# Attention's reload in eight buffers, and branch B's product begun with three tiles in places of their own

## The chip, the cores and the metric

The kernel runs on one core of one Trainium2 chip. The metric is the device time of one execution in microseconds, as the median of repeated runs. Beside it stands one profiled execution, from which every row below is taken. The engines are TensorE (PE, with its weight loads as PEld), VectorE (DVE), ScalarE (ACT), GpSimd (POOL) and SyncE (SP), which issues most of the transfers.

## The reference

One step of a one-layer streaming encoder with 1024 features: 528 prompt tokens (16 of them learned) and 64 sample tokens, so T = 592 columns. A normalised input goes through one wide projection, then through two branches side by side, a gated merge and an MLP. The lines that matter:

```python
h = _rmsnorm(x, p["norm1"])
proj = h @ p["w_in"]          # q, k, v of attention | DeltaNet q, k, v | z | beta, decay | gates A, B
o_a = attend(qa, ka, va, lam) # differential attention, two softmax maps per head
o_a = (_rmsnorm(o_a, p["sub_norm"]) * (1.0 - lam_init)).reshape(bsz, t, A_V_WIDTH)
...
o_b, s_new = _gated_delta(qb, kb, vb, g, beta, ssm0.astype(f32))
z = jax.nn.silu(z_b.astype(f32)).reshape(bsz, t, B_HEADS, B_HEAD_DIM)
o_b = (_rmsnorm(o_b, p["gdn_norm"]) * z).reshape(bsz, t, B_WIDTH).astype(x.dtype)
y_a = o_a @ p["w_br_a"]
y_b = o_b @ p["w_br_b"]
mix = jax.nn.sigmoid(gate_a + p["b_gate"][0]) * y_a + jax.nn.sigmoid(gate_b + p["b_gate"][1]) * y_b
x = x + mix @ p["w_out"]
h2 = _rmsnorm(x, p["norm2"])
x = x + jnp.square(jax.nn.relu(h2 @ p["w_up"])) @ p["w_down"]
```

## The kernel before

**Layout and arithmetic.** Activations lie with features on the partitions: eight tiles (KC = 8, index kc) of 128 features by TQ = 576 columns. Every product is made in three terms: a weight and an activation are each split into a rounded high part and a remainder (`split`, L275: ScalarE casts the high part, VectorE subtracts for the low part), and high x high, high x low and low x high are accumulated. A product task of 256 output features (`feat`, L470) has four parts, two halves of the features by two halves of 288 columns. A part is 8 x 3 = 24 matmuls into one bank; PG = 3 banks of the tag `pg` are used in turn. After a part its `evac` reads the bank, and the bank is free for the next part but two.

**Order.** The instructions of each engine's queue are written in the order in which a planner emits them (`manual_schedule`). The planner `Pace` (L53) keeps an estimated time per engine. `stream` (L300) walks through the list of tasks and yields after every 8 matmuls; `drive` (L449) lets it take one such step, then lets each side chain (a generator) take a step if the planner holds its inputs for ready. A task starts only when its `need` holds. Stores are put off until the planner holds their source for ready, and all transfers of the stages below, except the tiles of x, go through SyncE's queue in order.

**The stages that the change touches.** The last tasks that read the normalised input `hh`, `hl` are the gate tasks `g00` to `g03` (`gate_tasks`, L1175): each part ends in a tanh on ScalarE (`gt`), stored to `th_d`. Attention's chains run beside them. `load_ob` (L1430) loads DeltaNet's output from `ob_d` into eight tiles `ma` as soon as DeltaNet is through, then waits for the mark "hidden" and splits all eight into the place of `hh` and `hl`, which nobody reads any more, and sets "ob". The task `g03` is given `last=("hidden", "ob")`: after its last product it sets "hidden" and holds until "ob" is set, and only then emits its outstanding tanh.

Then come four tasks `bb0` to `bb3` (`br_b_tasks`, L1445; product of DeltaNet's output with `w_br_b`, tile `pg_bb`). Their `evac` loads a gate tile `thb`, multiplies on VectorE and stores to `mb_d`. HELD = 3: `bb0` to `bb2` need "ob"; `bb3` needs "merge", which is set when all of attention's chains are through and its memory has been given back. Attention's finished heads lie in `oa_d` by then. `load_oa` (L1489) loads them again, tile after tile through SyncE, into a tag `oa` with two buffers, and splits each into `oh` and `ol`; then "oa" is set. Four tasks `ba0` to `ba3` (`br_a_tasks`, L1465, tile `pg_ba`) need "oa". Their `evac` loads `tha` and `mbr` (branch B's result) and adds, and splits the sum into `mxh`, `mxl`. The tag `gth` has three buffers for `gt`, `thb`, `tha` and `mbr` together.

`residual` (L1497) runs from the end of `bb3` on: for each of five tiles of x it issues a load through GpSimd into a tag `xt` with one buffer, waits for the planner's landing time and 4000 ns more, turns it on TensorE in two groups (`pxr`) and copies to `x1`. When `ba3` and `residual` are through, the task `o0` (tile `pg_o`, the product with `w_out`) may start.

## Time and profile before

| | us |
|---|---|
| median of 3 runs | 1315.92 (1314.86 to 1316.42) |
| the profiled execution | 1314.69 |
| its span, first to last instruction | 1312.9 |
| TensorE busy | 1277.6 (97%) |
| VectorE busy | 863.8 (66%) |
| ScalarE busy | 603.7 (46%) |
| GpSimd busy | 110.1 (8%) |
| mean granted clock of TensorE | 0.994 |

The profiled execution's own time is 1.79 us above its span. "Busy" of TensorE counts a matmul from its start to its modelled end, so two that overlap in the pipeline are counted once. A granted clock of 1.00 is 2.4 GHz, of 0.50 it is 1.2 GHz. A wait is put down to the releaser that came last. Nearly all instructions pass through one helper, so all have the line L165; they are told apart by their tiles.

### The profile page before, as it was taken

Reading aid. Unit: us, or ns where it says so; the run is one execution under the profiler, and the core shown is the slowest. Engines: PE = TensorE matmul, PEld = TensorE weight load, DVE = VectorE, ACT = ScalarE, POOL = GpSimd, SP = SyncE. Lnnn points to the kernel's source line nnn. Section 1 sums busy time; section 2 is a strip of 40 time slices with the busy share of each in tenths; the row PEclk is TensorE's granted clock in tenths of the full one; section 3 lists DMA queues with packets and bytes.
Section 4 is the critical chain, followed back from the end, with each engine's and each line's share of the span. In section 5 each row is a group of like instructions: output and inputs, shape, how many; then the busy total and the mean of one; then the engine's idle time right before and its main releaser. Section 6 shows DMA issues by size and latency. Waiting matters only on the chain.

```text
span 1312.9 us, 25759 instructions
## 1 busy us (share of the span) xinstructions
PE 1277.6 (97%) x10177; PEld 1236.2 (94%) x10177; DVE 863.8 (66%) x1887; ACT 603.7 (46%) x1421; POOL 110.1 (8%) x207
## 2 busy tenths in 40 slices
PE   7999999999999999999998997999999999999998
PEld 5989899999999999998887997999999999999998
DVE  5766899434477624557777864445678678678687
ACT  5565554333643343237676652233453453453442
POOL 3111423200021000000000001200000000000000
PEclk9999999999999999999999998999999999999999
DMA  6324144532654422676444435632232323323322
GB/s 164 96 68 154 56 132 127 157 94 64 204 171 131 140 85 68 186 218 206 143 149 149 157 122 203 213 107 82 68 94 90 105 64 97 113 60 99 100 77 77
DMA packets 167934, 160.48 MB, mean 122 GB/s; under 512 B 24587, under 2 KB 148765, under 8 KB 167814
## 3 DMA queue, kind: packets, MB, share of 16 engines
q1 hardware_dynamic: 165702, 153.04, 38.3%
q0 software_dynamic: 2112, 5.80, 1.5%
q8 instruction: 80, 1.31, 0.4%
q14 instruction: 40, 0.33, 0.1%
HBM read 123.94 MB, written 37.81 MB: 123 GB/s over the span
## 4 chain that ended last, share of the span: by engine, by line
PE 85%; DVE 6%; ACT 4%; DMA 3%; issue 1%; SPq 0%; POOL 0%; DVEq 0%; ACTq 0%; POOLq 0%
PE pg_u L165 16%; PE pg_a L165 11%; PE pg_d L165 9%; PE pg_g L165 7%; PE pg_ba L165 4%; PE pg_z L165 4%; PE pg_o L165 4%; PE pd_dn L165 4%; PE pa_dn L165 4%; PE pc_dn L165 4%; PE pg_bb L165 3%; PE ppo L165 2%; PE pb_dn L165 2%; ACT djk L165 2%; PE po L165 1%
## 5 line engine op out<-in xcount | busy, mean ns | idle before, releaser
L165 PE MATMUL pg_u<-h2h,wh_u 128*128 128x288 f32 x512 | 151.4, 296 | 0.0
L165 PE MATMUL pg_u<-h2h,wl_u 128*128 128x288 f32 x512 | 151.3, 296 | 0.0
L165 PE MATMUL pg_u<-h2l,wh_u 128*128 128x288 f32 x512 | 151.3, 296 | 0.0
L165 PE MATMUL pg_a<-wh_a,hh 128*128 128x256 f32 (+1 forms) x480 | 136.3, 284 | 0.1
L165 PE MATMUL pg_a<-wh_a,hl 128*128 128x256 f32 (+1 forms) x480 | 135.8, 283 | 0.0
L165 PE MATMUL pg_a<-wl_a,hh 128*128 128x256 f32 (+1 forms) x480 | 135.5, 282 | 0.0
L165 PE MATMUL pg_d<-hl,wh_d 128*128 128x336 f32 (+1 forms) x384 | 115.5, 301 | 0.3 <-DVE hl L165 0.3
L165 PE MATMUL pg_d<-hh,wh_d 128*128 128x336 f32 (+1 forms) x384 | 115.6, 301 | 0.0
L165 PE MATMUL pg_d<-hh,wl_d 128*128 128x336 f32 (+1 forms) x384 | 115.4, 301 | 0.0
L165 PEld LDWEIGHTS pg_u<-h2h,wh_u 128*128 128x128 f32 x512 | 96.1, 188 | 0.1
L165 PEld LDWEIGHTS pg_u<-h2l,wh_u 128*128 128x128 f32 x512 | 96.1, 188 | 0.0
L165 PEld LDWEIGHTS pg_u<-h2h,wl_u 128*128 128x128 f32 x512 | 96.1, 188 | 0.0
L165 PEld LDWEIGHTS pg_a<-wh_a,hh 128*128 128x128 f32 (+1 forms) x480 | 86.5, 180 | 0.8 <-ACT sq L165 0.3
L165 PEld LDWEIGHTS pg_a<-wh_a,hl 128*128 128x128 f32 (+1 forms) x480 | 86.6, 181 | 0.5 <-issue 0.3
L165 PEld LDWEIGHTS pg_a<-wl_a,hh 128*128 128x128 f32 (+1 forms) x480 | 86.5, 180 | 0.3 <-issue 0.2
L165 PE MATMUL pg_g<-hh,wl_g 128*128 128x288 f32 x256 | 77.1, 301 | 0.0
L165 PE MATMUL pg_g<-hh,wh_g 128*128 128x288 f32 x256 | 77.0, 301 | 0.0
L165 PE MATMUL pg_g<-hl,wh_g 128*128 128x288 f32 x256 | 76.8, 300 | 0.0
L165 PEld LDWEIGHTS pg_d<-hl,wh_d 128*128 128x128 f32 x384 | 72.4, 189 | 1.2 <-issue 0.6
L165 PEld LDWEIGHTS pg_d<-hh,wl_d 128*128 128x128 f32 x384 | 72.8, 189 | 0.7 <-issue 0.6
L165 PEld LDWEIGHTS pg_d<-hh,wh_d 128*128 128x128 f32 x384 | 72.5, 189 | 0.2
L165 ACT CAST wh_dn<-wr_dn 128x1024 fp32r<-128x1024 f32 x32 | 33.6, 1050 | 81.4 <-DVE wr_dn L165 41.2
(398 smaller groups left out, 3785.0 us busy)
## 6 DMA issues: line engine op xcount, KB each, us to landing
wr_u<-in_w_up_dram SPq DMA_DIRECT2D x32, 512.0 KB, 3.6
wr_dn<-in_w_down_dram SPq DMA_DIRECT2D x32, 512.0 KB, 3.7
wr_d<-in_w_in_dram SPq DMA_DIRECT2D x24, 512.0 KB, 5.6
wr_a<-in_w_in_dram SPq DMA_DIRECT2D x24, 512.0 KB, 3.9
wr_g<-in_w_in_dram SPq DMA_DIRECT2D x16, 512.0 KB, 4.7
at_d<-st SPq DMA_DIRECT2D x48, 128.0 KB, 2.4
th_d<-gt SPq DMA_DIRECT2D x16, 288.0 KB, 2.1
wr_z<-in_w_in_dram SPq DMA_DIRECT2D x8, 512.0 KB
```

Source lines behind the costliest of these rows:

```text
L165: r = f(*a, **kw)
```

## The change

Four things are changed.

- `load_oa`: the eight tiles `oa` have a buffer each, and all eight loads are issued at once through GpSimd's queue when the merge's memory is opened. The chain only splits, tile after tile.
- `load_ob` and `feat`: the first OWN = 3 tiles of DeltaNet's output are split into a new pool `own`, without waiting for "hidden"; only the other five wait for it. `bb0` is called with `lead=3`: it first emits the matmuls of these three tiles for three parts, in three banks, and then completes each part with the remaining five tiles.
- `feat`: an outstanding `evac` is emitted before a task sets its `last` mark and holds, not after. Only `g03` has such a mark among the tasks that use `feat`, so its last tanh stands ahead of the splits.
- `residual`: two buffers for the tiles of x, the next load is issued one tile ahead, and the first turning waits until the first two parts of `ba0` are evacuated.

```diff
--- before.py
+++ after.py
@@ -45,6 +45,7 @@
 SC = 3
 WT = 2
 HELD = 3
+OWN = 3
 MASKED = -32768.0
 
 THR = [0, 1, 2, 3, 4, 5, 6, 7, 8, 12, 16, 23, 32, 46, 64, 91]
@@ -467,18 +468,29 @@
                     c.ready, idle = r or pace.ready, 0
         pace.flush()
 
-    def feat(xh, xl, nm, evac, m=P, ms=(0, P), halves=QHALVES, after="start", last=None, turn=False):
+    def feat(xh, xl, nm, evac, m=P, ms=(0, P), halves=QHALVES, after="start", last=None, turn=False, lead=0):
 
         def body(w):
             parts, full = [(h, c) for h in range(len(ms)) for c in (halves[::-1] if turn and h else halves)], deque()
             if "start" not in done:
                 parts.sort(key=lambda x: x[1])
+
+            begun = {}
+            for h, (a, b) in parts[:PG if lead else 0]:
+                ps = begun[h, a] = pg.tile([P, 512], F32, name=f"pg_{nm}{h}{a}", tag="pg")
+                for kc in range(lead):
+                    for i, (ww, xx) in enumerate(((w[0], xh), (w[0], xl), (w[1], xh))):
+                        TE.matmul(ps[:m, :b - a], ww[:, kc, ms[h]:ms[h] + m], xx[kc][:, a:b], start=kc == i == 0, stop=False)
+                yield
             for h, (a, b) in parts:
                 while len(full) == PG:
                     yield False
-                ps = pg.tile([P, 512], F32, name=f"pg_{nm}{h}{a}", tag="pg")
-                n = 0
-                for kc in range(KC):
+                ps = begun.pop((h, a), None)
+                k0 = 0 if ps is None else lead
+                if not k0:
+                    ps = pg.tile([P, 512], F32, name=f"pg_{nm}{h}{a}", tag="pg")
+                n = 3 * k0
+                for kc in range(k0, KC):
                     for ww, xx in ((w[0], xh), (w[0], xl), (w[1], xh)):
                         xk = xx[kc] if isinstance(xx, list) else xx[:, kc]
                         TE.matmul(ps[:m, :b - a], ww[:, kc, ms[h]:ms[h] + m], xk[:, a:b], start=n == 0, stop=n == 3 * KC - 1)
@@ -486,12 +498,12 @@
                         if n % QUANTUM == 0 and n < 3 * KC:
                             yield
                 full.append((h, ps[:m, :b - a], a, b))
+                while full and after in done:
+                    evac(*full.popleft())
                 if last and h == len(ms) - 1 and b == TQ:
                     done.add(last[0])
                     while last[1] not in done:
                         yield False
-                while full and after in done:
-                    evac(*full.popleft())
                 yield
         return body
 
@@ -598,7 +610,7 @@
     hh = hp.tile([P, KC, T], F32R, name="hh")
     hl = hp.tile([P, KC, T], F32R, name="hl")
     hq, lq = (x[:, :, N0:T] for x in (hh, hl))
-    ob = [x[:, :, 0:TQ] for x in (hh, hl)]
+    ob = [[], []]
 
     def load_x(pl, t):
         xt = pl.tile([P, D], F32, name=f"x_s{t}", tag="xt")
@@ -1436,10 +1448,17 @@
             obs.append(ab_.tile([P, TQ], F32, name=f"ma{j}", tag="ob"))
             Q.dma_start(obs[j], ob_d[j][:, N0:T])
             yield
+        for j in range(OWN):
+            for o in ob:
+                o.append(late["own"].tile([P, TQ], F32R, name=f"own{j}{len(ob[0])}", tag=f"own{j}{len(o)}{o is ob[0]}"))
+            split(ob[0][j], ob[1][j], obs[j])
+            yield
         while "hidden" not in done:
             yield
-        for j in range(KC):
-            split(ob[0][:, j], ob[1][:, j], obs[j])
+        for j in range(OWN, KC):
+            for o, x in zip(ob, (hh, hl)):
+                o.append(x[:, j, 0:TQ])
+            split(ob[0][j], ob[1][j], obs[j])
         done.add("ob")
 
     def br_b_tasks():
@@ -1456,7 +1475,7 @@
                     store(mb_d[j], th)
 
             def body(w, c=c, evac=evac):
-                yield from feat(ob[0], ob[1], f"bb{c}", evac)(w)
+                yield from feat(ob[0], ob[1], f"bb{c}", evac, lead=OWN if c == 0 else 0)(w)
                 if c == 3:
                     done.add("br_b")
             out.append(Task(f"bb{c}", w_br_b[0], c * 256, body, has("ob") if c < HELD else has("merge")))
@@ -1476,6 +1495,7 @@
                 if b == TQ:
                     V.tensor_tensor(th, th, mb, ALU.add)
                     split(late["mxh"][j], late["mxl"][j], th)
+                    done.add(f"ba{j}")
 
             def body(w, c=c, evac=evac):
                 yield from feat(late["oh"], late["ol"], f"ba{c}", evac)(w)
@@ -1487,19 +1507,28 @@
     late = {}
 
     def load_oa():
-        for j in range(KC):
-            a = mg.tile([P, TQ], F32, name=f"oa{j}", tag="oa")
-            Q.dma_start(a, oa_d[j])
-            yield
+        for a in late["oa"]:
+            yield pace.free(a)
+            j = late["oa"].index(a)
             split(late["oh"][j], late["ol"][j], a)
         done.add("oa")
 
     def residual():
 
         x1 = late["x1"]
-        for t, (c0, n) in enumerate(QTILES):
-            xt = mg.tile([P, D], F32, name=f"x_r{t}", tag="xt")
-            G.dma_start(xt[:n], x_prompt[0, c0:c0 + n] if t < 4 else x_sample[0])
+        xts = deque()
+        for t in range(-1, NT):
+            if t < NT - 1:
+                c0, n = QTILES[t + 1]
+                xts.append(mg.tile([P, D], F32, name=f"x_r{t + 1}", tag="xt"))
+                G.dma_start(xts[-1][:n], x_prompt[0, c0:c0 + n] if t < 3 else x_sample[0])
+            if t < 0:
+
+                while "ba0" not in done:
+                    yield
+                continue
+            c0, n = QTILES[t]
+            xt = xts.popleft()
             yield pace.free(xt) + 4000
             for q in range(2):
                 pv = bank(f"pxr{t}{q}").rearrange("p (k c) -> p k c", k=4)
@@ -1686,6 +1715,8 @@
         chains += [Chain(delta(g)) for g in range(2)]
         chains.append(Chain(conv_out()))
         drive(lambda: not chains and has("delta0", "delta1")())
+    own_cm = pool("own")
+    late["own"] = own_cm.__enter__()
     with pool("attn", side="right") as at_:
         ab_ = Tags(pace, at_, qk=4, v=3, past=3, sc=SC, mx=6, wT=WT, ob=8, aoss=3, bias=2, osb=3,
                    aqT0=2, aqT1=2, akT0=2, akT1=2)
@@ -1697,12 +1728,16 @@
         for nm in ("mxh", "mxl"):
             late[nm] = [mp.tile([P, TQ], F32R, name=f"{nm}{j}", tag=f"{nm}{j}") for j in range(KC)]
         with pool("merge", side="right") as mg_:
-            mg = Tags(pace, mg_, oa=2, xt=1)
+            mg = Tags(pace, mg_, oa=8, xt=2)
+            late["oa"] = [mg.tile([P, TQ], F32, name=f"oa{j}", tag="oa") for j in range(KC)]
+            for j in range(KC):
+                G.dma_start(late["oa"][j], oa_d[j])
             for nm in ("oh", "ol"):
                 late[nm] = [mg.tile([P, TQ], F32R, name=f"{nm}{j}", tag=f"{nm}{j}") for j in range(KC)]
             done.add("merge")
             chains.append(Chain(load_oa()))
             drive(has("br_b"))
+            own_cm.__exit__(None, None, None)
             hp_cm.__exit__(None, None, None)
             xp = ctx.enter_context(pool("x1"))
             late["wx"] = Tags(pace, xp)
```

## Rows read from the trace of the kernel before

**Rows 1.** The page: the span; engines' busy time, share of it, instructions.

```profile
span 1312.9 us, 25759 instructions
...
PE 1277.6 (97%) x10177; PEld 1236.2 (94%) x10177; DVE 863.8 (66%) x1887; ACT 603.7 (46%) x1421; POOL 110.1 (8%) x207
```

**Rows 2.** Stretches, PE alone: from:to, length, busy (count), PEclk, DMA share, GB/s.

```profile
798.55:815.00 16.45, 8.80 (x36) 0.69 0.48 159
785.50:797.60 12.10, 12.10 (x93) 1.00 0.90 306
805.00:814.00 9.00, 5.36 (x16) 0.50 0.46 148
```

**Rows 3.** Timeline of SyncE (start, us, engine, line, what); the tile `oa`'s issues, ns min/median/max.

```profile
800.32 0.32 SPq L165 DMA_DIRECT2D mb_d<-thb  x1
800.74 7.53 SPq L165 DMA_DIRECT2D oa<-oa_d  x4
...
L165 SPq DMA_DIRECT2D oa<-oa_d x8: 319/410/1066, 784.1 to 807.9; - x8
```

**Rows 4.** Timeline of ScalarE and TensorE; in brackets the idle time before, and its releaser.

```profile
805.75 1.37 ACT L165 CAST oh<-oa 128x576 fp32r<-128x576 f32 x2 [5.70 <-DMA oa<-oa_d]
...
806.47 0.61 PE L165 MATMUL pg_ba<-oh,wh_ba 128*128 128x288 f32 x1 [4.92 <-ACT oh L165]
```

**Rows 5.** Stretches, PE alone, columns as in group 2.

```profile
705.95:721.10 15.15, 11.51 (x76) 0.89 0.42 130
592.00:705.90 113.90, 113.17 (x904) 1.00 0.51 162
709.00:712.00 3.00, 3.00 (x14) 0.50 0.01 2
```

**Rows 6.** Timeline of ScalarE, VectorE and TensorE, 704 to 720 us.

```profile
706.89 4.67 ACT L165 CAST hh<-ma 128x576 fp32r<-128x576 f32 x8
711.47 0.49 ACT L165 ACTIVATE gt<-pg_g,bgh 128x288 f32<-128x288 f32 x1
...
707.58 5.44 DVE L165 TENSOR_TENSOR hl<-ma,hh 128x576 fp32r<-128x576 f32 x8 [0.23 <-ACT hh L165]
...
707.60 0.40 PE L165 MATMUL pg_bb<-hh,wh_bb 128*128 128x288 f32 x1 [1.67 <-ACT hh L165]
719.31 0.33 PE L165 MATMUL ptk<-ident,k 128*128 128x128 f32 x1 [1.60 <-DVE mx L165]
```

**Rows 7.** Tile `x_r`: issues (ns min/median/max), landing; timeline of GpSimd at 786 us.

```profile
L165 POOL DMA_DIRECT2D x_r<-in_x_prompt_dram x4: 547/561/610, 788.5 to 835.2; - x4
...
DMA to landing us min/median/max: 3.9/4.7/4.8
...
786.21 2.40 POOL L165 TENSOR_TENSOR wl_ba<-wr_ba,wh_ba 128x1024 fp32r<-128x1024 f32 x1 [24.39 <-ACT wh_ba L165]
```

**Rows 8.** Chain of waits in order of time, 774 to 800 us: start, us, what.

```profile
782.20 0.64 PE pot L165 x5
782.84 8.76 PE pg_bb L165 x64
...
793.67 4.95 DMA thb<-th_d
```

**Rows 9.** Chain of waits, 818 to 866 us: turnings of x, the next product.

```profile
830.86 0.44 PE pxr L165 x4
...
844.53 0.44 PE pxr L165 x4
...
858.78 0.39 PE pxr L165 x4
...
865.76 0.27 PE pg_o L165 x2
```

**Rows 10.** Stretches, all engines: length, then PE, PEld, DVE, ACT, POOL busy (count), PEclk, DMA.

```profile
600.00:620.00 20.00, 19.84 (x160) 17.41 (x159) 15.26 (x52) 13.88 (x48) 0.61 (x4) 1.00 0.56 182
...
760.00:780.00 20.00, 19.87 (x157) 18.23 (x157) 14.12 (x56) 10.26 (x31) 0.15 (x1) 1.00 0.25 85
```

## Prediction

> **What bounds the kernel now.** I read the page first: TensorE is busy for 1277.6 of the 1312.9 us of the span [rows 1]. A part of this kernel is therefore worth what it takes away from TensorE's idle or slow time, and work of the other engines counts only where TensorE waits for it. Second, I looked with the view by stretches for places where TensorE's busy time or its granted clock falls below full. In the part that the diff touches there are two. From 798.55 to 815.00, where the product of branch A begins, there are 36 recorded matmuls in 16.45 us at a mean clock of 0.69, against 93 in 12.10 us just before [rows 2]. From 705.95 to 721.10, where the product of branch B begins, there are 76 matmuls in 15.15 us, against 904 in 113.90 us in the stretch before, with nearly the same mixture of a product and attention [rows 5]. Third, I read the timeline for what ended each wait.
>
> In the first place SyncE issues a store of `thb` at 800.32, and only behind it, at 800.74, the remaining reloads of the attention output; four issues take 7.53 us because each needs one of two buffers back from a split [rows 3]. ScalarE's split stands idle for 5.70 us until the transfer lands, and TensorE for 4.92 us until that split [rows 4]. The clock goes to 0.50 afterwards, which is the 1.2 GHz level, for about nine microseconds [rows 2]. In the second place ScalarE makes all eight splits in a row from 706.89 (4.67 us, 0.58 each) and VectorE their low parts from 707.58 (5.44 us, 0.68 each). TensorE has waited 1.67 us for the first, and the clock is 0.50 from 709 to 712. The last gate's tanh comes at 711.47, behind all of them. At 719.31 TensorE waits another 1.60 us for VectorE, which has not caught up [rows 5, 6].
>
> **The sum against the profiled execution.** It took 1314.69 us, which is the span of 1312.9 and 1.79 around it; it lies 1.23 us below the median of the runs shown, 1315.92. I take the gain from the profiled time and add these 1.23 us again.
>
> **Reload in eight buffers, issued by GpSimd.** A matmul of a clean stretch costs 12.10 / 93 = 0.130 us, so the 36 of the bad one should take 4.7 us, and 16.45 - 4.7 = 11.8 us are lost now [rows 2]. This includes the slow clock, which I therefore don't count again. The change removes the waiting for two buffers and takes eight issues out of SyncE's queue, where they stood behind the stores of branch B. It adds eight issues to GpSimd's queue at 0.56 us each, or 4.5 us; a load from that queue landed in 3.9 to 4.8 us [rows 7]. When do they start? At the earliest when the destination's memory is free; at the latest when attention's last output is stored. TensorE turns this last output until 782.8, and I allow 3.3 us for the copy and the store [rows 8]. From 786.1 the last of eight would be issued by 790.6 and landed by 795.4, and its two halves of the split (0.58 and 0.68) are done by 796.7. Branch A's product starts at 798.55 [rows 2]. So even the late case fits, with 1.9 us to spare, and the kc that needs the last split comes 21 matmuls (2.7 us) later. In the early case seven of eight land before attention ends. I take 11.5 us as the gain. The bounds are 12 and 6.5: the low one is a transfer of 4.95 us, as `thb` has now [rows 8], that would come back on the path.
>
> Queued behind the eight issues on GpSimd are one subtraction that makes low weights (`wl_ba`, 2.40 us at 786.21 [rows 7]) and the first load of x. SyncE's next load of weights waits for that subtraction, and a load of `thb` stands behind the load of weights. Up to 4.5 us of delay there is covered: the weights in question are those of the second of four steps, due 96 matmuls (12.5 us) after 798.55; a late `thb` holds a bank that is needed 24 matmuls (3.1 us) after 798.55. I cost it at nothing; uncovered it costs 4.5 - 3.1 = 1.4 us.
>
> A rule speaks against this part. The Trainium skill says (Trainium Kernel Development and Optimization, Key Constraints) that transfers issued from several engines share the same 16 DMA engines, and that issuing from another engine saves only the sequencer's issue time. By that rule the change of queue would win about 8 x 0.41 us of issuing [rows 3], so some 3.3 us in place of 11.5, and the time would be 1309.1. The trace agrees on the sharing (the share of 0.90 below) but not that the issue time is all: at 800.74 it is a store and a buffer that SyncE's queue waits for [rows 3].
>
> **Three tiles early, three banks, tanh first.** Counted with the 113.90 / 904 = 0.126 us per matmul of the mixed stretch, the 76 matmuls should take 9.6 us, so 15.15 - 9.6 = 5.5 us are lost [rows 5]: 1.67 of waiting for the first tile, about 2.2 of slow clock and small waits, 1.60 for VectorE. With three tiles split long before, 3 banks x 3 tiles x 3 matmuls = 27 matmuls (3.5 us) can run from 705.95. Meanwhile ScalarE ends its attention work at 706.9, makes the tanh (0.49) and five splits of 0.58: all high parts by 710.3. VectorE's five low parts end at about 711.4. TensorE reaches the fourth tile at about 709.5 and the last at 711.2; some 0.3 us of waiting stay. The third bank is freed by the tanh at about 707.4, and it is needed after 18 matmuls, at 708.3. So the first 3.9 us should go. The 1.60 us for VectorE need not: VectorE has 3 x 0.68 = 2.0 us less to do there, but TensorE arrives 3.9 us earlier, so this wait can also grow by 1.9 us. Gain between 5.5 + 0.5 (if attention is also served better) and 2.0; I take 3.5, nearer to the row with the remaining wait.
>
> The three splits go to the stretch in which DeltaNet's output is reloaded, near 600 to 620. There ScalarE is busy for 13.88 and VectorE for 15.26 of 20 us, with TensorE at 19.84 [rows 10]: 3 x 0.58 and 3 x 0.68 fit. I cost them at nothing; without that cover they cost 2 us. The matmuls stay the same in number, and moving tanh in `feat` changes no other task.
>
> **Residual after branch A's first step, two buffers.** Now a tile of x is turned every 13.7 us (830.86 to 844.53), and the last is turned at 858.78, 7 us before the next product starts at 865.76 [rows 9]. The change starts this later, after two parts of the first step (48 matmuls, 6.3 us), but loads a tile ahead. Only the transfer and the fixed delay in the order (4 us) are overlapped; I estimate a step of about 10 us, so 6.3 + 4 x 10 + 4 = 50 us, against 96 x 4 x 0.130 + 4 = 54 us for the product with its turning. It costs nothing then.
>
> The sum: 11.5 + 3.5 = 15.0 us. 1314.69 - 15.0 = 1299.7, and at the median of runs 1300.9.
>
> **Rivals.**
> - The start's gain is given back at the merge. Branch B's fourth step may not start before attention's chains are through. Now that is tight: attention's last turning ends at 782.84, and the fourth step, 96 x 0.130 = 12.5 us long and over by about 797.8, begins near 785.3, only 2.5 us later; 64 matmuls of branch B run without a break in between and behind [rows 8]. If attention goes at its own speed (VectorE is busy for 15.26 of 20 us near 600 [rows 10]), branch B's first three steps run out 3.5 us sooner and TensorE waits there instead. For it: 64 matmuls in a row show attention not ready, or through, for a long piece [rows 8]. Against it: VectorE has 2 us less to do. Time: 1304.4.
> - Transfers. From 785.5 to 797.6 the DMA engines are busy for 0.90 of the time [rows 2]. If the reloads don't start before attention's end, five of them (1.47 MB, 4.8 us at the 306 GB/s of that stretch) are added there, and `thb`, weights or `tha` come 5 us late on the path: 1305.9. Against it: from 760 to 780 the share is 0.25 [rows 10], and seven of eight outputs are stored by then. With the first rival together, 1309.4. The skill's rule above ends at the same place.
> - Slower: the residual becomes the bound. If a tile still takes 13.7 us, since what sets it may be the order and not the buffer, the last one is turned 6.3 + 4 x 13.7 + 4 = 65.1 us after the start, and the next product waits 11 us for it, with the slow clock behind that wait (nine microseconds at half speed cost 4.5). That takes away 15.6 us: 1316.5. With the 3.5 us of the first rival lost besides, it is slower: 1320. The residual decides from a step of 11 us per tile on.
> - The change doesn't do what it says: the early splits are placed late in the order, or the eight loads wait for memory on GpSimd until attention's last tiles are free. The second is the late case reckoned above and costs nothing. The first leaves the start as it is: 1304.4 again.
>
> **How the numbers follow.** Forecast, 1300.9 with 1297 to 1303 of its own: 0.58. Gain of the start lost in either way, 1304.4: 0.19. Transfers (with the page's rule, 1306 to 1309.5): 0.12. Residual as the bound: 0.11, half of it within the 0.2% (2.6 us, about what a measurement of this kernel can tell from no change) and half beyond. The range reaches from 1315.92 - 12 - 6 = 1297.9, taken down to 1297 because both losses are reckoned from recorded matmuls alone and a few records can be missing, to the joint case of 1309.5. Faster 0.89, same 0.05, slower 0.06.
>
> **What would show it.** Right: no row of `oa` in SyncE's queue; eight issues on GpSimd with all landings before branch B's last matmul; no wait of TensorE over 0.5 us at the first product of branch A; a granted clock of 1.00 in both places; 27 matmuls right behind the last gate, and the tanh ahead of five splits. Wrong: TensorE idle ahead of branch B's fourth step (the merge); a wait for `tha` or `thb`; the last turning of x just before `pg_o`; or a new wait near 600. If both places are clean and the time is still above 1305, the loss lies where I didn't look.

## The result, and the profile after

The changed kernel takes **1324.59 us** (median of 4 runs, 1321.59 to 1325.15) against 1315.80 of the kernel before beside it. The ratio is 1.0058, 95% interval 1.0036 to 1.0080: it is slower by 8.8 us, where 1300.9 was forecast. The profiled execution took 1321.59. The page of the changed kernel answers [rows 1]:

```profile
span 1319.8 us, 25749 instructions
...
PE 1282.1 (97%) x10177; PEld 1240.0 (94%) x10177; DVE 863.2 (65%) x1883; ACT 603.6 (46%) x1423; POOL 117.9 (9%) x217
```

The change touches only what lies between attention's first score matmul (`psc`) and the first matmul of `pg_o`. Three marks cut that into two stages: **stage A** from the first `psc` to the first `pg_ba` (gates, attention, branch B), **stage B** from there to the first `pg_o` (branch A). The view by stretches gives it for the kernel before, with the three stretches gates, branch B and branch A (columns: from:to, length, busy us and count of PE, PEld, DVE, ACT, POOL, then PEclk, DMA share, GB/s):

```profile
591.40:707.60 116.20, 113.81 (x912) 101.58 (x911) 88.03 (x327) 83.60 (x260) 5.16 (x36) 1.00 0.52 164
707.60:798.00 90.40, 88.16 (x673) 81.10 (x674) 63.94 (x213) 50.43 (x141) 4.89 (x16) 0.98 0.48 158
798.60:865.60 67.00, 59.35 (x419) 56.88 (x418) 29.23 (x41) 20.51 (x30) 13.70 (x8) 0.92 0.57 184
```

and for the changed kernel:

```profile
590.00:698.00 108.00, 105.36 (x838) 94.12 (x837) 78.35 (x275) 74.01 (x225) 4.25 (x30) 1.00 0.51 164
698.00:807.10 109.10, 100.12 (x748) 89.97 (x747) 75.15 (x263) 63.31 (x182) 12.94 (x31) 0.95 0.44 142
807.10:872.50 65.40, 58.68 (x426) 57.73 (x426) 27.84 (x40) 17.54 (x25) 15.21 (x9) 0.95 0.59 193
```

Stage A grew by 9.9 us (207.2 to 217.1), stage B fell by 1.6 only (67.0 to 65.4); what follows takes 447.3 us in both, and the first `psc` came 1.4 earlier (591.4, 590.0). 9.9 - 1.6 - 1.4 = 6.9 us, the difference of the two spans. The gates' stretch became 8.2 us shorter, but only since 74 recorded matmuls left it; 75 more stand in branch B's, which takes 18.1 us more (the line of before ends 0.6 us short of the first `pg_ba`). There TensorE is idle for 9.0 us (2.2 before), and its clock is 0.95 (0.98 before). Over all of stage A idle time grew by 7.0 us (4.6 to 11.6). The other 2.9 us are longer busy time of nearly as many recorded matmuls, at a lower mean clock.

**The start** is as forecast. TensorE's timeline at the end of the gates has no wait left; the tiles `own` follow attention's matmuls directly (before: 1.67 us [rows 6]):

```profile
696.52 0.61 PE L166 MATMUL ppo<-v,wT 128*128 128x128 f32 x4
697.06 1.00 PE L166 MATMUL psc<-akT,aqT 64*128 64x264 f32 x12
697.98 0.53 PE L166 MATMUL pg_bb<-own,wh_bb 128*128 128x288 f32 x2
```

**The merge's wait** is new. From 767 to 792 attention is alone on TensorE, since branch B's first three steps are used up and the fourth may not begin (`pwT` turns the softmax weights, `ppo` multiplies them by v, `pot` turns the finished output):

```profile
769.30 1.23 PE L166 MATMUL pwT<-ident,sc 128*128 128x128 f32 x5 [1.88 <-DVE sc L166]
...
778.35 1.01 PE L166 MATMUL pwT<-ident,sc 128*128 128x128 f32 x7 [0.95 <-DVE mx L166]
...
781.71 1.83 PE L166 MATMUL ppo<-v,wT 128*128 128x128 f32 x14 [1.46 <-ACT wT L166]
...
790.86 1.38 PE L166 MATMUL pot<-ident,osb 128*128 128x128 f32 x5 [2.54 <-DVE osb L166]
```

Where [rows 8] had 64 matmuls of branch B without a break, TensorE now waits for softmax steps one by one. The last turning (`pot`) ends at 792.2, before at 782.8.

**The reload** has moved its wait. GpSimd's timeline, then SyncE's, VectorE's and TensorE's, answer [rows 3, 4]:

```profile
787.47 2.12 POOL L166 DMA_DIRECT2D oa<-oa_d  x4 [9.99 <-PE ppo L166]
795.43 0.54 POOL L166 DMA_DIRECT2D oa<-oa_d  x1 [5.84 <-DMA oa_d<-oaT]
800.05 0.54 POOL L166 DMA_DIRECT2D oa<-oa_d  x1 [4.08 <-DMA thb<-th_d]
800.61 4.77 POOL L166 TENSOR_TENSOR wl_ba<-wr_ba,wh_ba 128x1024 fp32r<-128x1024 f32 x2
...
812.28 2.34 POOL L166 TENSOR_TENSOR wl_ba<-wr_ba,wh_ba 128x1024 fp32r<-128x1024 f32 x1 [1.68 <-ACT wh_ba L166]
...
803.05 2.73 SPq L166 DMA_DIRECT2D wr_ba<-in_w_br_a_dram  x2
805.84 0.50 SPq L166 DMA_DIRECT2D thb<-th_d  x1
...
801.30 6.04 DVE L166 TENSOR_TENSOR ol<-oa,oh 128x576 fp32r<-128x576 f32 x3
811.94 0.45 DVE L166 SCALAR_TENSOR_TENSOR thb<-thb,pg_bb 128x288 f32<-128x288 f32 x1 [4.60 <-DMA thb<-th_d]
812.31 3.59 DVE L166 TENSOR_TENSOR ol<-oa,oh 128x576 fp32r<-128x576 f32 x2
...
815.29 0.61 PE L166 MATMUL pg_ba<-ol,wh_ba 128*128 128x288 f32 x1 [6.72 <-DVE ol L166]
```

Read it from the end. TensorE waits 6.72 us for a low part `ol`. That subtraction itself takes 2.92 us (0.75 is usual): it runs beside a subtraction of GpSimd from 812.28 to 814.62. So some 2.2 of the 6.72 us are VectorE's slow pace there. VectorE has it behind the multiplication of `thb`, for which it waits 4.60 us. SyncE has issued this `thb` only at 805.84, behind two loads of weights, and these need the raw weights' place back from GpSimd's two subtractions, which end at 805.4. GpSimd could not begin them before the eighth load was issued. The seventh load had waited 5.84 us for a store of attention's output. The eighth reads what the last store writes, which SyncE issued at 796.17; the releaser shown is the load of `thb` that SyncE issued 0.37 us behind it. The reload itself is in time: ScalarE's last high part `oh` is done at 804.0, 3 us ahead of the first `pg_ba` at 807.07:

```profile
L166 ACT CAST oh<-oa x8: 675/680/688, 797.9 to 803.3; 128x576 fp32r<-128x576 f32 x8
```

**The residual** is at its new pace: its last turning of x stands at 856, 16 us ahead of `pg_o`, where [rows 9] had 7 us.

### The profile page after: what moved, and what is told of

It is laid out like the page before. It is cut to its first block, busy times and chain, and to the rows that moved or that the text cites. A ratio compares the mean times of both kernels' runs of the same rounds, so it can differ in the third digit from the quotient of the medians.

```text
span 1319.8 us, 25749 instructions
## 1 busy us (share of the span) xinstructions
PE 1282.1 (97%) x10177; PEld 1240.0 (94%) x10177; DVE 863.2 (65%) x1883; ACT 603.6 (46%) x1423; POOL 117.9 (9%) x217
## 4 chain that ended last, share of the span: by engine, by line
PE 81%; DVE 5%; DMA 5%; ACT 4%; issue 3%; POOL 1%; SPq 1%; DVEq 0%; POOLq 0%; ACTq 0%
PE pg_u L166 16%; PE pg_a L166 11%; PE pg_d L166 9%; PE pg_g L166 5%; PE pg_ba L166 5%; PE pg_z L166 4%; PE pg_o L166 4%; PE pd_dn L166 4%; PE pa_dn L166 4%; PE pc_dn L166 4%; PE pg_bb L166 2%; PE pb_dn L166 2%; PE ppo L166 2%; DMA bias_d<-bv_d 2%; PE po L166 1%
## 5 line engine op out<-in xcount | busy, mean ns | idle before, releaser
L166 DVE SCALAR_TENSOR_TENSOR cv_d<-pre_d,vec,cv_d 128x595 f32<-128x595 f32 x72 | 61.6, 861 | 14.7 <-ACT cv_d L166 7.9
```

The costliest lines, as they stand in the source:

```text
L166: r = f(*a, **kw)
```

## Experiments

All runs in one table. "A" and "B" are the stages of the profiled execution; the ratio is to the kernel before on the same chip.

| kernel | median us | ratio, 95% interval | A | B |
|---|---|---|---|---|
| before | 1315.80 | | 207.2 | 67.0 |
| the change | 1324.59 | 1.0058 (1.0036 to 1.0080) | 217.1 | 65.4 |
| start_only | 1330.26 | 1.0113 (1.0095 to 1.0130) | 218.3 | 71.3 |
| reload_only | 1318.00 | 1.0025 (1.0013 to 1.0037) | 207.9 | 67.8 |
| after_athidden | 1311.19 | 0.9971 (0.9954 to 0.9988) | 205.9 | 63.8 |
| after_sp | 1323.26 | 1.0064 (1.0042 to 1.0085) | 217.0 | 64.0 |
| reload_res | 1310.32 | 0.9955 (0.9939 to 0.9971) | 207.0 | 64.2 |
| reload_res_v | 1303.21 | 0.9916 (0.9893 to 0.9940) | 206.4 | 56.4 |
| athidden_v | 1305.10 | 0.9920 (0.9897 to 0.9943) | 206.0 | 56.4 |
| late2_v | 1310.80 | 0.9965 (0.9948 to 0.9982) | 212.8 | 57.1 |
| before_v | 1319.64 | 1.0026 (1.0013 to 1.0039) | 207.1 | 69.8 |
| after_v | 1316.59 | 1.0012 (0.9994 to 1.0029) | 216.6 | 57.1 |
| after_lead0 | 1317.84 | 1.0019 (1.0007 to 1.0031) | 211.8 | 65.1 |
| best | 1304.59 | 0.9918 (0.9902 to 0.9933) | 206.8 | 56.4 |
| charge2_v | 1314.19 | 0.9984 (0.9973 to 0.9995) | 218.7 | 57.1 |
| unch_v | 1307.24 | 0.9926 (0.9910 to 0.9941) | 210.6 | 57.1 |
| charge_v | 1307.80 | 0.9943 (0.9925 to 0.9962) | 209.2 | 57.9 |

The first `psc` lies between 589.0 and 595.2 us in these executions, in stages that no edit touches. The stages A and B are therefore steadier than the totals: kernels that are alike up to the merge agree within 1.7 us in A (206.4 to 207.9 with the order of before, 216.6 to 218.3 with that of the change).

**First four: which half loses.** Theory W: the early splits change the order that the planner writes, attention stands further back, and TensorE waits at the merge. Counted in the written queue of TensorE, 198 of 288 `psc` stand ahead of the last gate matmul before, 162 in the change; the last `pot` stands behind 272 of branch B's 384 matmuls before, behind 288 in the change. Rival Q: the time is lost in GpSimd's queue behind the eight loads. `start_only` is the change with reload and residual of before (first diff, against the change); `reload_only` is the kernel before with the reload alone (second diff).

```diff
-            mg = Tags(pace, mg_, oa=8, xt=2)
...
+            mg = Tags(pace, mg_, oa=2, xt=1)
```

```diff
-            mg = Tags(pace, mg_, oa=2, xt=1)
+            mg = Tags(pace, mg_, oa=8, xt=1)
+            late["oa"] = [mg.tile([P, TQ], F32, name=f"oa{j}", tag="oa") for j in range(KC)]
+            for j in range(KC):
+                G.dma_start(late["oa"][j], oa_d[j])
```

> The start alone (three early tiles, three banks, tanh first); reload and residual as before. Theory W: in the written order of the changed kernel attention stands further back (162 of 288 score matmuls ahead of the last gate matmul, 198 before), so branch B's first three steps run out and TensorE waits for attention's tail at the merge; this kernel then is no faster than the kernel before, 1314 to 1326 us, with TensorE idle ahead of branch B's fourth step. Rival Q: the time is lost in GpSimd's queue, behind the eight loads; then this kernel shows the start's gain, 1309 to 1313 us.

> The eight buffers and the loads from GpSimd alone; start and residual as before (198 score matmuls ahead of the last gate matmul). Theory W: the reload's gain comes, 1304 to 1309 us, no wait over 2 us at branch A's first product. Rival Q: the subtraction for low weights and SyncE's loads stand behind the eight loads, 1314 to 1320 us.

The start alone costs 15.0 us beside its own runs of before (1315.30), more than the whole change and above W's range. Its TensorE waits at the merge as the change's does, and the reload's stall of before stands behind it:

```profile
772.55 0.77 PE L166 MATMUL pwT<-ident,sc 128*128 128x128 f32 x5 [1.87 <-DVE sc L166]
...
795.74 1.03 PE L166 MATMUL pot<-ident,osb 128*128 128x128 f32 x5 [2.53 <-DVE osb L166]
```

The reload alone gains nothing: W fell there, and Q's mechanism, subtractions behind the last load, is in its trace, TensorE and then GpSimd:

```profile
805.41 0.61 PE L165 MATMUL pg_ba<-ol,wh_ba 128*128 128x288 f32 x1 [6.25 <-DVE ol L165]
...
864.02 1.09 PE L165 MATMUL pxr<-ident,x_r 64*128 64x64 f32 x8 [3.79 <-DMA x_r<-in_x_sample_dram]
...
787.96 0.54 POOL L165 DMA_DIRECT2D oa<-oa_d  x1 [7.75 <-DMA oa_d<-oaT]
788.51 4.77 POOL L165 TENSOR_TENSOR wl_ba<-wr_ba,wh_ba 128x1024 fp32r<-128x1024 f32 x2
```

The second line shows a third loss: with the old residual the last tile of x is now what ends branch A.

Then the change with its three `own` tiles split together with the other five, the lead kept, and the change with the eight loads issued by SyncE:

```diff
+        while "hidden" not in done:
+            yield
         for j in range(OWN):
...
-            yield
```

```diff
-                G.dma_start(late["oa"][j], oa_d[j])
+                Q.dma_start(late["oa"][j], oa_d[j])
```

> The changed kernel, but its three tiles in places of their own are split only when the last gate has been written, with the other five; three banks and tanh first are kept. The written order ahead of the merge is that of the kernel before (198 score matmuls). Theory W: 1303 to 1309 us, no wait at the merge. Rival Q: 1315 to 1320 us.

> The changed kernel with the eight loads issued by SyncE in place of GpSimd. Theory W: the wait at the merge stays, 1317 to 1325 us. Rival Q: the loss is gone, 1304 to 1312 us.

Splitting late brings 13.4 us and the written order of before (198, 272); TensorE waits 2.06 us at the start again, and not at the merge. The queue of the loads alone is worth 1.3 us, inside the scatter. The Trainium skill (Trainium Kernel Development and Optimization, Key Constraints) says that issuing from several engines saves only the sequencer's issue time; this pair agrees, with 1.3 us between the two queues. The reload isn't late in `after_sp` (the last high part begins at 801.8, branch A at 806.8), and GpSimd's first two subtractions no longer stand behind the loads (793.23, not 800.61). Yet TensorE waits twice at branch A, 4.86 us together, each time for a low part `ol` that VectorE makes in 2.9 us beside a subtraction of GpSimd; VectorE, GpSimd, TensorE:

```profile
808.00 5.76 DVE L166 TENSOR_TENSOR ol<-oa,oh 128x576 fp32r<-128x576 f32 x2
...
807.99 5.16 POOL L166 TENSOR_TENSOR wl_ba<-wr_ba,wh_ba 128x1024 fp32r<-128x1024 f32 x2 [9.48 <-ACT wh_ba L166]
...
811.00 0.40 PE L166 MATMUL pg_ba<-ol,wh_ba 128*128 128x288 f32 x1 [2.71 <-DVE ol L166]
813.82 0.61 PE L166 MATMUL pg_ba<-ol,wh_ba 128*128 128x288 f32 x1 [2.15 <-DVE ol L166]
```

So the low weights on GpSimd hurt by two routes: late, behind the loads, and as a brake on VectorE's subtractions beside them.

**Second four: three losses priced.** Theory N: (a) the early splits, (b) the low weights on GpSimd behind the eighth load, (c) the old residual. Rival T: the DMA engines are too full for the reload. Rival E: an early split costs wherever it is put. `reload_res` adds the change's part of `residual` and its mark "ba0" to `reload_only`, with `xt=2`; `_v` means this edit besides, by which no low weights are made on GpSimd between the opening of the merge's memory and the tail:

```diff
     def VG(out, n):
 
-        if "tail" in done or "attn" in done and "merge" not in done:
+        if "attn" in done:
             return V
```

> The eight buffers with GpSimd's loads, and the residual's new place and second buffer; start as before. Theory N has three losses: (a) the early splits push attention back in the written order; (b) low-weight subtractions on GpSimd stand behind the eighth load and hold SyncE's loads, so that thb comes late and VectorE's low parts of the attention output stand behind it; (c) with the reload earlier, the residual as it was becomes the bound (in the run with the reload alone the last turning of x ended at 864.8 and the next product began at 865.0, 5.8 us after branch A's last matmul). N expects (c) gone here: 1307 to 1312 us. Rival T: the DMA engines are too full in this stretch, and what is taken from one wait goes to another: 1315 to 1320 us.

> The same, and all low-weight subtractions from the attention stage on go to VectorE, so that nothing stands behind the eight loads on GpSimd but the loads of x. Theory N: (b) is gone, 1302 to 1307 us, the longest wait at branch A's first product under 2 us. Rival T: transfers stay late, no gain over the run without this edit, 1309 to 1313 us.

(c) is 7.7 us by the medians: 3.6 in stage B, and 2.3 in slow clock behind the wait for x, since from the first `pg_o` on `reload_only` takes 449.6 us and not 447.3. (b) is 7.1 us, and stage B is 7.8 shorter. The same transfers run in both, so T fell. But the edit does more than take two subtractions out from behind the loads. In `reload_res` the first of them begins at 789.16, only 3.0 us later than before; TensorE's wait of 5.49 us is for an `ol` that VectorE begins after waiting 5.07 us for `thb`, and that takes 2.90 us beside GpSimd. With `_v` the brake is gone, and SyncE's queue is written otherwise: the last two loads of `thb` (from 786.48) stand ahead of the loads of weights (791.18), where the last one stood behind them (794.37). The 7.1 us are the price of all this together; no run divides it. The rows of `reload_res`, VectorE, GpSimd, TensorE:

```profile
801.98 0.46 DVE L165 SCALAR_TENSOR_TENSOR thb<-thb,pg_bb 128x288 f32<-128x288 f32 x1 [5.07 <-DMA thb<-th_d]
802.35 4.24 DVE L165 TENSOR_TENSOR ol<-oa,oh 128x576 fp32r<-128x576 f32 x3
...
802.30 2.34 POOL L165 TENSOR_TENSOR wl_ba<-wr_ba,wh_ba 128x1024 fp32r<-128x1024 f32 x1 [0.83 <-ACT wh_ba L165]
...
805.31 0.61 PE L165 MATMUL pg_ba<-ol,wh_ba 128*128 128x288 f32 x1 [5.49 <-DVE ol L165]
```

With both edits branch A is clean: 427 matmuls busy for 56.49 of 56.50 us at full clock, in the stretch view:

```profile
796.80:853.30 56.50, 56.49 (x427) 55.56 (x426) 29.28 (x42) 17.55 (x25) 1.58 (x3) 1.00 0.59 189
```

67.0 - 56.5 = 10.5 us is what the reload's stall was worth.

> The changed kernel with its three tiles split at the last gate (written order of attention as before) and the low-weight subtractions on VectorE. Theory N: 1302 to 1307 us, below the 1311.2 of the run that left them on GpSimd. Rival T: 1309 to 1313 us.

`late2_v` splits the three tiles when the task `g02` begins:

```diff
+            def body(w, inner=inner, c=c):
+                if (which, c) == (0, 2):
+                    done.add("own")
+                yield from inner(w)
...
+        while "own" not in done:
+            yield
         for j in range(OWN):
```

> As the run before, but the three tiles are split early, at the start of the last gate task but one: 198 score matmuls ahead of the last gate matmul as before the change, 228 and 270 after the first and second step of branch B (234 and 288 before the change). Theory N: the wait at the start is gone and a short wait at the merge comes, 1300 to 1307 us. Rival E: an early split costs wherever it is put, since TensorE's wait at the start was what let attention catch up; 1309 to 1318 us, with TensorE idle ahead of branch B's fourth step.

The lead with late splits is worth nothing beside `reload_res_v` (206.0 against 206.4 in stage A). For `late2_v` Rival E held (stage A is 6.4 us longer). It keeps 198 `psc` ahead of the gates' end and takes the start's wait away, and TensorE gives it back at the merge, with 288 matmuls of branch B (before 272) ahead of the last turning:

```profile
707.20 0.71 PE L166 MATMUL pwT<-ident,sc 128*128 128x128 f32 x5
707.67 0.52 PE L166 MATMUL pg_bb<-own,wh_bb 128*128 128x288 f32 x2
...
788.15 1.41 PE L166 MATMUL pot<-ident,osb 128*128 128x128 f32 x5 [5.68 <-DVE osb L166]
```

**Third four: controls.** The edit `_v` on the kernel before (`before_v`) and on the change (`after_v`); the change without the lead (first diff); and `reload_res_v` with the tanh moved, without early splits and lead (second diff).

```diff
-                yield from feat(ob[0], ob[1], f"bb{c}", evac, lead=OWN if c == 0 else 0)(w)
+                yield from feat(ob[0], ob[1], f"bb{c}", evac, lead=0)(w)
```

```diff
+                while full and after in done:
+                    evac(*full.popleft())
                 if last and h == len(ms) - 1 and b == TQ:
...
-                while full and after in done:
-                    evac(*full.popleft())
```

> The kernel before, with one edit: the low parts of weights that are made between the opening of the merge's memory and the tail are made by VectorE and none by GpSimd. It is the control for the pair of runs in which that edit took 7 us. Theory N (GpSimd's two subtractions are late only because they stand behind eight loads in GpSimd's queue): before has no loads there, its reload stall is set by two buffers and SyncE's queue, so 1313 to 1318, no change. Rival D (those subtractions slow VectorE whatever stands ahead of them, and taking them off GpSimd is a gain of its own): 1306 to 1311.

> The changed kernel as it is, with the low parts of weights after the merge's memory is open made by VectorE. Theory N: inside the whole change the second loss is worth what it was beside the reload alone, about 7 us, and the merge's waits stay as they are, so 1315 to 1320; the matmul behind branch A's first splits waits less than 1 us. Rival M (with attention late anyway, the reload ends late for the last output's store, and the subtractions are hidden behind that wait): 1321 to 1325, and ScalarE's or VectorE's last splits still end branch A's wait.

> The changed kernel with the three tiles still split early, but branch B's product beginning as in the kernel before (no first three tiles in three banks). In the written order attention still stands back (162 of 288 score matmuls ahead of the last gate matmul; 216, 234, 288 at the end of branch B's first three steps, where the change has 198, 228, 252). Theory W (the early splits push attention back, and the lead does little to that): the merge's wait is there as in the change, 1320 to 1327, and the start's stall is there again or halved. Rival L (it is the lead, which takes three banks and turns 27 matmuls at once, that pushes attention back): 1308 to 1314.

> The reload by GpSimd in eight buffers, the new residual, the low weights by VectorE after the merge's memory is open, and the tanh moved ahead of the splits; no early splits and no lead. The written order of attention is that of the kernel before. Theory N: nothing at branch A, the start as in the kernel before but for the tanh, which frees a bank earlier and can take away the 0.39 us wait for a bank at the most: 1300 to 1304. Rival S (the tanh ahead of the splits delays the first split that TensorE waits for by its 0.5 us): 1304 to 1306.

The edit `_v` is no gain of its own: on the kernel before it costs 4 us, and neither expectation held (stage B grows by 2.8, with a third wait for a high part `oh`, 1.58 us at 816.21; why was not followed). Inside the change it is worth 8.0 us, as N said. In the kernel before no `ol` stands beside a subtraction of GpSimd (its longest takes 0.76 us), so neither route was there to be removed. Early splits and lead form a square in stage A, all with the new reload and residual (the first without the tanh moved, which gains nothing in `best`): neither 207.0, lead alone 205.9, early splits alone 211.8, both 217.1. The early splits cost 4.8, the lead 5.3 more on top of them, and nothing by itself. The total of `after_lead0` lies between the two expectations, and so does its cause: the early splits bring a wait of 2.44 us for the last turning, and only with the lead do the waits of the change appear. `best` equals `reload_res_v` within the scatter, and the tanh ahead of the splits gains nothing: TensorE waits 2.05 us for its first split, 1.66 there, as Rival S said. Both are 0.8% faster than the kernel before.

**Last three: load or order.** The early splits could cost by their work on ScalarE and VectorE or by the planner's order. `charge2_v` is `athidden_v` with the planner's clocks moved on where the change splits, without a split there; `unch_v` is `after_v` with real early splits and the planner's clocks put back; `charge_v` moves the clocks on at another moment.

```diff
+        for j in range(OWN):
+            pace.t["ACT"] = max(pace.t["ACT"], pace.free(obs[j])) + 571
+            pace.t["DVE"] = max(pace.t["DVE"], pace.t["ACT"] + 60) + 672
+            yield pace.t["DVE"] + 100
         while "hidden" not in done:
```

```diff
+            t0 = dict(pace.t)
             split(ob[0][j], ob[1][j], obs[j])
+            pace.t.update(t0)
```

> The kernel with all eight splits at the end of the gates and the low weights by VectorE, but the planner's clocks of ScalarE and VectorE are moved on by three splits at the moments at which the change makes them; no instruction is made early. The written order has attention as far back as with real early splits and no lead (162 of 288 score matmuls ahead of the last gate matmul; 216, 234, 288 at the ends of branch B's first three steps). Theory W (the written order costs the time): the stretch from the first score matmul to branch A is 211 to 217 us, 1310 to 1317 in all, with a wait of TensorE for attention at the merge. Rival E (the load of the early splits on the engines costs it): that stretch is 205 to 207 as in the kernel that splits at the end of the gates, 1303 to 1306.

> The change with the low weights by VectorE, and the three early splits made where the planner has them, but without moving its clocks on for them. The written order at the end of the gates is that of the kernel before (198), and 216, 258, 288 at the ends of branch B's first three steps. Theory W: attention stands nearly as before, so the stretch from the first score matmul to branch A is 205 to 210 us, 1302 to 1308 in all; of the start's gain of some 3 us a part is given back at the merge, since 16 more matmuls of branch B stand ahead of attention's last turning. Rival E: 211 to 217 us, 1309 to 1317.

> As the first of these three, but the planner's clocks are moved on for the three splits at once, as soon as the first tile of DeltaNet's output is there. The written order at the end of the gates is that of the kernel before (198), and attention's last turning stands further ahead (behind 256 of branch B's matmuls; before 272). Theory W: no wait at the merge, and nothing gained either, since none was left there: stretch 205 to 207 us, 1302 to 1306. Rival F (any charge in the planner costs time): above 1308.

`charge2_v` and `athidden_v` do the same work; the written order differs (162 against 198), and stage A is 218.7 against 206.0 us. No engine does anything early. TensorE is idle for 12.8 us in the stage (4.6 in `athidden_v`), and its mean clock is 0.97 (0.99). The waits are not those of the change: 3.21 us stand at the start, 2.17 in branch B's first step and 4.1 at the merge, where the change has 7.1:

```profile
700.07 0.61 PE L166 MATMUL pg_bb<-own,wh_bb 128*128 128x288 f32 x1 [3.21 <-ACT own L166]
...
727.60 0.66 PE L166 MATMUL pwT<-ident,sc 128*128 128x128 f32 x4 [2.17 <-DVE mx L166]
...
784.73 1.38 PE L166 MATMUL ppo<-v,wT 128*128 128x128 f32 x10 [0.82 <-ACT wT L166]
...
791.49 1.38 PE L166 MATMUL pot<-ident,osb 128*128 128x128 f32 x5 [3.32 <-DVE osb L166]
```

So the written order alone can cost as much as the change lost (the total is in W's range, the stage even above it); E's explanation by load alone fell. `unch_v` shows it from the other side: it differs from `after_v` in the planner's clocks alone, has 198, and its stage A is 210.6 against 216.6 us. These 6.0 us are the order's. The 4.2 that remain above `reload_res_v` it does not divide: its stage lies just above W's range, and TensorE waits around 630, where the planner did not count the splits, and at the merge a little (2.76 us), where 288 matmuls of branch B still stand ahead of the last turning:

```profile
628.57 0.77 PE L166 MATMUL pwT<-ident,sc 128*128 128x128 f32 x5 [0.99 <-DVE sc L166]
...
633.73 0.83 PE L166 MATMUL pot<-ident,osb 128*128 128x128 f32 x4 [1.05 <-DVE osb L166]
635.50 0.27 PE L166 MATMUL pot<-ident,osb 64*128 64x64 f32 x1 [0.95 <-DVE mx L166]
```

`charge_v` missed its range a little (209.2 and 1307.80): no wait at the merge, but 4.70 us ahead of the first product of branch B. Moving the planner's clocks at another moment does not push attention back at all, so what the planner does with three splits is not in proportion to them. Why it turns some 2 us of charge into 36 score matmuls was not followed further.

## Why the prediction was wrong

**What bounds the kernel: right.** Both stalls were real, and the reload's had the size read: its 11.8 us lost are 10.5 in the clean kernels. But the forecast's gain of 11.5 was the size of the stall, not what this change takes away: stage B became 1.6 us shorter. The start's 3.5 us turned into a loss of 9.9 in stage A.

**"I cost it at nothing" for GpSimd's queue: the first step that failed.** The low weights on GpSimd hold 8.0 us of the change (`after_v`; 8.3 in stage B), where 1.4 was the uncovered price. The chain was named up to `thb`, but the step asked only for which bank a late `thb` holds. It did not ask what stands behind `thb` on VectorE: the low parts `ol`, which branch A needs first. Nor did it ask what GpSimd's subtractions do to VectorE's beside them: an `ol` takes 2.9 us there, not 0.75. In `after_sp`, with the loads out of GpSimd's queue, two such `ol` make up some 4.3 of the 4.86 us that TensorE waits. The queue's own delay was reckoned rightly. The last load was issued 7.8 us after attention's last turning (800.05 and 792.24), as in the forecast's late case (790.6 and 782.8); it is attention that was 9.4 us late. "The second is the late case reckoned above and costs nothing" was thus right for the loads, and wrong for what stands behind them.

**"I cost them at nothing" for the three early splits: the second step that failed,** and the larger one: with the lead they cost 9.9 us in stage A. The room on the engines [rows 10] was there: in the change TensorE is idle for 2.6 us in the gates' stretch, 2.4 before. (Only `unch_v`, where the planner doesn't count the splits, waits 4.1 us between 628 and 651 against 0.3 before.) What was not asked is what the planner does with the splits. It writes the order by its own clocks, so moving a step re-times everything that it emits after it. Of the 10.2 us by which stage A of `after_v` exceeds that of `reload_res_v`, 6.0 go when only the planner's clocks are put back (`unch_v`).

**The first rival named the right place, with the wrong size.** It left attention where it was and priced the merge at the loss of the start's 3.5 us. In the change attention's last turning ends 9.4 us later (792.2, before 782.8). In `late2_v`, with attention nearly in its old order, stage A is 6.4 us longer than in `reload_res_v` (212.8 against 206.4); with the order of the change it is 10 longer. Every kernel here without a wait at the start has a stage A over 210 us. The reading that fits is that branch B's first three steps are what fills TensorE until attention is through, and that a start without a wait only uses them up sooner; it is read from the waits at the merge and not tested by itself. No run here kept the start's gain of 3.5 us.

**The residual at nothing: right.** A tile takes about 7 us (the first turning at 827.3, the last at 856.0), below the 10 estimated, and `reload_only` shows what the third rival described, but with the old residual. The transfers' rival was not the cause by itself, since `reload_res_v` makes the same transfers, issued in another order, without a wait; a late `thb` was still what one saw.

**The range failed** because each loss in it was bounded by the gain that it could cancel. A reordering is not so bounded: the change's stage A is longer by nearly three times the start's gain. The one slower case that was named, the residual as the bound, did not come.

## What to carry to other kernels

When a planner writes the order, compare the written order of the engine that bounds the kernel before and after (how far the long chain stands ahead at each stage's end) before pricing anything by engine time. Before removing a stall on the busiest engine, ask whether the chain that it waits for at the next join also gets earlier; in seven kernels here the stall was gone and the join no sooner. When loads move to another engine's queue, take the last one's inputs: whatever stands behind it on that queue now waits for them too, and each thing that it releases is to be followed to its own engine's queue. Where work moves between GpSimd and VectorE, look also at what then runs beside it.

## What the hardware showed beside

A low part `ol` takes 0.75 us on VectorE. Beside a GpSimd subtraction of weights it ends only about 0.6 us after that one: those above took 2.9 us, and one, beside two subtractions in a row (800.61 to 805.38), took 4.70. The view of the tile in the changed kernel (ns min/median/max, first and last start):

```profile
L166 DVE TENSOR_TENSOR ol<-oa,oh x8: 745/746/4701, 801.3 to 817.5; 128x576 fp32r<-128x576 f32 x8
```

With the low weights on VectorE (`reload_res_v`) the longest is 0.752 us. The Trainium skill (SBUF — State Buffer, Who interferes with whom) says that a VectorE instruction with two inputs in SBUF contends with a GpSimd instruction that reads SBUF, and that the port pair they share is an exclusive lock. The trace agrees, and shows that two GpSimd instructions in a row can hold one of VectorE (4.70 us).
